# Max pooling over groups of 16: sixteen full loads, the last one pooled by four halving maxima

## The chip, the cores and the metric

The kernel runs on one core of one Trainium2 chip. The metric is device time in microseconds (us) for one execution, input and output in the chip's main memory (HBM). The engines that matter here are VectorE (DVE), which does the pooling; SyncE (SP) and ScalarE (ACT), which only issue transfers; and the 16 DMA engines, which move the bytes. On-chip memory has 128 partitions, and one instruction of DVE works on all partitions side by side.

## The reference

The reference is an adaptive max pooling of `x` with shape 32 x 256 x 4096 to 256 outputs per row. Since 4096 is a multiple of 256, every output is the maximum of 16 neighbouring values.

```python
for i in range(output_size):                      # 256
    start = int(i * length / output_size)         # 16 * i
    end = int((i + 1) * length / output_size)     # 16 * (i + 1)
    result[:, :, i] = np.max(x[:, :, start:end], axis=-1)
```

So 134.2 MB are read, 8.39 MB are written, and all values are float32.

## The kernel before, in words

All rows are one long sequence of groups of 16 values: 2,097,152 groups, 16,384 for each of the 128 partitions. A load of CHUNK = 1024 groups for each partition is 64 KB per partition and 8,192 KB in all. The sequence is cut into two large stretches, GROUPS = (9, 6): nine loads in the first, and six full loads, one load of 896 groups and one of 128 in the second. Within a stretch a partition owns consecutive groups, so that a store can take the results of many loads at once.

There is one on-chip tile `sb`. Its first RING elements hold the input of the loads, its rest the results. The ring has room for two loads, each with a gap of GAP = 152 groups beside it. Load k goes to half k % 2; every other time it is moved by the gap (`moved`, line 86). Load k+2 lies over load k but for 152 groups of it, and in their place it uses the gap. Load k is pooled in two pieces, the large one of 872 groups first and then the small one of 152 (lines 92 to 95), so load k+2 may start as soon as the large piece of load k is done. Two loads are in flight or queued at any time.

Order of the work: SP issues a short load of 128 groups (FIRST, line 70), then fifteen full loads and the last of 896 groups (line 88), all in one queue, each held back until the large piece of the load two before it is pooled. DVE pools in the same order, each piece by one `reduce_max` over the 16 values (line 57). The short load is pooled first and alone (line 73); its 128 results lie right behind the place where the 896 results of the last load go (line 98), so that one store of ACT (line 100) writes the last 1024 groups of each partition. `tc.no_sync_barrier()` makes no engine wait: it only keeps the stores behind it in the order of the program. Then SP issues the two large stores (line 103), 4,608 KB for the nine loads and 3,072 KB for the six. The first can go as soon as its nine loads are pooled, so it stands in the queue right behind the last load; the second has to wait for DVE's small piece of the last full load.

There is no hand-written planner. The waits follow from the overlap of the regions of `sb`, and the order on each engine is that of the program.

Of the kernel before, what the change touches and what calls it, by code (L numbers as in the profile page):

```python
# [1 line left out]

# [4 lines left out]


@with_exitstack
def kernel(  # L10
    ctx: ExitStack,
    tc: tile.TileContext,
    x: bass.AP,
    output_size: bass.AP,
    out: bass.AP,
):
    nc = tc.nc
    P = nc.NUM_PARTITIONS
    fp32 = mybir.dt.float32

    B, C, L = x.shape
    O = int(output_size)
    assert L % O == 0, (L, O)
    W = L // O
    total = B * C * O // P
    assert B * C * O % P == 0

    xw = x.flatten_outer_dims().rearrange("r (o w) -> (r o) w", w=W)
    ow = out.flatten_outer_dims().rearrange("r o -> (r o)")
    taken = 0  # L30

    def group(n):

        nonlocal taken
        span = slice(taken * P, (taken + n) * P)
        taken += n
        return (
            xw[span].rearrange("(p n) w -> p (n w)", p=P),
            ow[span].rearrange("(p n) -> p n", p=P),
        )  # L40

    CHUNK = 1024
    GAP = 152
    FIRST = 128
    RING = 2 * (CHUNK + GAP) * W


    GROUPS = (9, 6)
    last = CHUNK - FIRST
    assert (sum(GROUPS) + 1) * CHUNK == total and last * (W + 1) <= CHUNK * W  # L50


    pool = ctx.enter_context(tc.tile_pool(name="pool", bufs=1))
    sb = pool.tile([P, RING + total - last], fp32, tag="sb", name="sb")

    def pooled(dst, at, n):
        nc.vector.reduce_max(  # L57
            out=sb[:, dst : dst + n],
            in_=sb[:, at * W : (at + n) * W].rearrange("p (n w) -> p n w", w=W),
            axis=mybir.AxisListType.X,  # L60
        )

    groups = [
        group((loads + (g == len(GROUPS) - 1)) * CHUNK) for g, loads in enumerate(GROUPS)
    ]
    assert taken == total
    x_end, o_end = groups[-1]
    cut = GROUPS[-1] * CHUNK

    nc.sync.dma_start(  # L70
        out=sb[:, CHUNK * W : (CHUNK + FIRST) * W], in_=x_end[:, (cut + last) * W :]
    )
    pooled(RING, CHUNK, FIRST)

    rows, stores = [], []
    at = RING + FIRST
    for (xg, og), loads in zip(groups, GROUPS):
        rows += [(xg, k * CHUNK, CHUNK, at + k * CHUNK) for k in range(loads)]
        if loads:
            stores.append((og[:, : loads * CHUNK], sb[:, at : at + loads * CHUNK]))  # L80
        at += loads * CHUNK
    rows.append((x_end, cut, last, None))

    for k, (xg, a, n, dst) in enumerate(rows):

        moved = k // 2 % 2
        at = k % 2 * (CHUNK + GAP) + moved * GAP
        nc.sync.dma_start(
            out=sb[:, at * W : (at + n) * W], in_=xg[:, a * W : (a + n) * W]
        )  # L90
        if dst is not None:
            mid = CHUNK - GAP if moved else GAP
            parts = [(0, mid), (mid, n)]
            for u, v in parts if moved else parts[::-1]:
                pooled(dst + u, at + u, v - u)
        else:
            assert (at + CHUNK) * W == RING
            pooled(RING - n, at, n)

    nc.scalar.dma_start(out=o_end[:, cut:], in_=sb[:, RING - last : RING + FIRST])  # L100
    tc.no_sync_barrier()
    for dst, src in stores:
        nc.sync.dma_start(out=dst, in_=src)


# [1 line left out]
_INS = ['x', 'output_size']  # L107
_OUTS = [((32, 256, 256), 'float32')]

_NUMBERS = {'output_size': 256}  # L110


# [26 lines left out]
```

## Time and profile before

| | us |
|---|---|
| median of 3 runs | 334.76 (334.68 to 334.80) |
| the profiled execution, its own time | 334.95 |
| its span, first to last instruction | 333.2 |
| DVE busy | 276.5 |
| first landing (short load, 1,024 KB), after its issue at 0.72 | 5.0 |
| the last load: issued 291.39, to landing | 21.6 |
| ACT's store: issued 328.34, to landing | 4.0 |

The page gives the busy time of each engine as a share of the span, and the load of the DMA queues: q1 is SP's (17 loads and two stores), q10 ACT's (one store). Times in the trace count from the start of the span. A share of 1.00 in the DMA column means that the 16 DMA engines were busy throughout. The chain of waits follows the work that ended last back from the end, and names for every step what released it.

Cut into 40 equal slices, the span looks like this (each digit is the busy share of a slice in tenths); the pattern is one load after the other:

```profile
DVE  2009979797997979799797979979797997979994
POOL 0000000000000000000000000000000000000000
DMA  9898989899898989899898989999898989999997
```

### The profile page before, as it was taken

The page shows a single profiled execution, that of the slowest core. Times are in us where ns is not written, and L with a number is a line of the kernel's source. Part 1 is how long each engine was busy: PE and PEld are TensorE (multiplying, and loading weights), DVE is VectorE, ACT ScalarE, POOL GpSimd, SP SyncE. Part 2 cuts the span into 40 slices and gives each one's busy share as a digit, 9 for nine tenths or more (in the row PEclk, how much of TensorE's full clock was granted, in tenths as well). Part 3 has the DMA queues.
Part 4 walks back from the last instruction along what each step waited for, and adds up shares of the span by engine and source line. Part 5 has one row for each costly group of instructions (what it writes and reads, how often), then busy time and mean ns, then how long its engine had stood idle before and what let it go on. Part 6 is the DMA issues. An engine that isn't in the chain of part 4 may idle for free.

```text
span 333.2 us, 113 instructions
## 1 busy us (share of the span) xinstructions
DVE 276.5 (83%) x32; POOL 0.2 (0%) x4
## 2 busy tenths in 40 slices
DVE  2009979797997979799797979979797997979994
POOL 0000000000000000000000000000000000000000
DMA  9898989899898989899898989999898989999997
GB/s 378 378 504 378 504 378 496 386 409 472 378 504 378 504 378 496 386 409 472 378 504 378 504 378 488 393 409 472 378 504 378 504 378 488 393 456 434 396 406 323
DMA packets 2880, 142.61 MB, mean 428 GB/s; under 512 B 320, under 2 KB 320, under 8 KB 448
## 3 DMA queue, kind: packets, MB, share of 16 engines
q1 hardware_dynamic: 2736, 142.08, 98.8%
q10 hardware_dynamic: 144, 0.52, 0.4%
HBM read 134.22 MB, written 8.39 MB: 428 GB/s over the span
## 4 chain that ended last, share of the span: by engine, by line
DMA 58%; DVE 36%; DVEq 5%; issue 0%; SPq 0%
DMA sb<-in_x_dram 58%; DVE sb L57 36%; DVEq L134 5%; SPq L70 0%
## 5 line engine op out<-in xcount | busy, mean ns | idle before, releaser
L57 DVE TENSOR_REDUCE sb<-sb 128x872 f32<-128x13952 f32 (+3 forms) x32 | 276.5, 8681 | 51.8 <-DMA sb<-in_x_dram 51.8
L120 POOL MEMSET const-bfloat16-1.0<- 128x1 bf16 x1 | 0.1, 102 | 0.0
L120 POOL MEMSET const-uint8-127<- 128x1 uint8 x1 | 0.1, 101 | 0.0
L120 POOL MEMSET const-float32-0.0<- 128x1 f32 x1 | 0.1, 99 | 0.2 <-issue 0.2
L120 POOL MEMSET const-float32-1.0<- 128x1 f32 x1 | 0.1, 98 | 0.0
## 6 DMA issues: line engine op xcount, KB each, us to landing
sb<-in_x_dram SPq DMA_DIRECT2D x1, 7168.0 KB, 21.6
out_dram<-sb SPq DMA_DIRECT2D x1, 4608.0 KB, 32.1
out_dram<-sb SPq DMA_DIRECT2D x1, 3072.0 KB, 17.7
sb<-in_x_dram SPq DMA_DIRECT2D x1, 1024.0 KB, 5.0
out_dram<-sb ACTq DMA_DIRECT2D x1, 512.0 KB, 4.0
sb<-in_x_dram SPq DMA_DIRECT2D x15, 24.0
```

Source lines behind the costliest of these rows:

```text
L57: nc.vector.reduce_max(out=sb[:, dst : dst + n], in_=sb[:, at * W : (at + n) * W].rearrange("p (n w) -> p n w", w=W), axis=mybir.AxisListT ...
L120: nc = _bacc.Bacc("TRN2", target_bir_lowering=False, num_devices=1)
L134: with _tile.TileContext(nc) as tc:
```

## The change

The short load and its pooling are taken out. GROUPS becomes (9, 7), and all sixteen loads have 1024 groups. The first fifteen are pooled as before, each in two pieces by `reduce_max`. The sixteenth is pooled by the new function `halved`, as a whole and in place: a maximum of the first eight values of each group with the last eight, written over the first eight; then four with four, two with two, and one with one. The last writes the 1024 results to the first elements of the ring, which are free by then (the load lies in the second half of the ring, and the load before it does not reach down there). ACT stores these 1024 results, and SP's two stores have the same sizes as before.

```diff
--- before.py
+++ after.py
@@ -41,66 +41,65 @@
 
     CHUNK = 1024
     GAP = 152
-    FIRST = 128
     RING = 2 * (CHUNK + GAP) * W
 
-
-    GROUPS = (9, 6)
-    last = CHUNK - FIRST
-    assert (sum(GROUPS) + 1) * CHUNK == total and last * (W + 1) <= CHUNK * W
+    GROUPS = (9, 7)
+    assert sum(GROUPS) * CHUNK == total and sum(GROUPS) % 4 == 0 and CHUNK <= GAP * W
 
 
     pool = ctx.enter_context(tc.tile_pool(name="pool", bufs=1))
-    sb = pool.tile([P, RING + total - last], fp32, tag="sb", name="sb")
+    sb = pool.tile([P, RING + total - CHUNK], fp32, tag="sb", name="sb")
+
+    def taps(at, n):
+        return sb[:, at * W : (at + n) * W].rearrange("p (n w) -> p n w", w=W)
 
     def pooled(dst, at, n):
         nc.vector.reduce_max(
-            out=sb[:, dst : dst + n],
-            in_=sb[:, at * W : (at + n) * W].rearrange("p (n w) -> p n w", w=W),
-            axis=mybir.AxisListType.X,
+            out=sb[:, dst : dst + n], in_=taps(at, n), axis=mybir.AxisListType.X
         )
 
-    groups = [
-        group((loads + (g == len(GROUPS) - 1)) * CHUNK) for g, loads in enumerate(GROUPS)
-    ]
-    assert taken == total
-    x_end, o_end = groups[-1]
-    cut = GROUPS[-1] * CHUNK
+    def halved(dst, at, n):
 
-    nc.sync.dma_start(
-        out=sb[:, CHUNK * W : (CHUNK + FIRST) * W], in_=x_end[:, (cut + last) * W :]
-    )
-    pooled(RING, CHUNK, FIRST)
+        win = taps(at, n)
+        w = W // 2
+        while w > 1:
+            nc.vector.tensor_max(win[:, :, :w], win[:, :, :w], win[:, :, w : 2 * w])
+            w //= 2
+        nc.vector.tensor_max(
+            sb[:, dst : dst + n].unsqueeze(2), win[:, :, :1], win[:, :, 1:2]
+        )
 
     rows, stores = [], []
-    at = RING + FIRST
-    for (xg, og), loads in zip(groups, GROUPS):
-        rows += [(xg, k * CHUNK, CHUNK, at + k * CHUNK) for k in range(loads)]
-        if loads:
-            stores.append((og[:, : loads * CHUNK], sb[:, at : at + loads * CHUNK]))
+    at = RING
+    for loads in GROUPS:
+        xg, og = group(loads * CHUNK)
+        rows += [(xg, k * CHUNK, at + k * CHUNK) for k in range(loads)]
+        stores.append((og, at, loads * CHUNK))
         at += loads * CHUNK
-    rows.append((x_end, cut, last, None))
 
-    for k, (xg, a, n, dst) in enumerate(rows):
+    for k, (xg, a, dst) in enumerate(rows):
 
         moved = k // 2 % 2
         at = k % 2 * (CHUNK + GAP) + moved * GAP
         nc.sync.dma_start(
-            out=sb[:, at * W : (at + n) * W], in_=xg[:, a * W : (a + n) * W]
+            out=sb[:, at * W : (at + CHUNK) * W], in_=xg[:, a * W : (a + CHUNK) * W]
         )
-        if dst is not None:
+        if k < len(rows) - 1:
             mid = CHUNK - GAP if moved else GAP
-            parts = [(0, mid), (mid, n)]
+            parts = [(0, mid), (mid, CHUNK)]
             for u, v in parts if moved else parts[::-1]:
                 pooled(dst + u, at + u, v - u)
         else:
-            assert (at + CHUNK) * W == RING
-            pooled(RING - n, at, n)
 
-    nc.scalar.dma_start(out=o_end[:, cut:], in_=sb[:, RING - last : RING + FIRST])
+            assert moved
+            halved(0, at, CHUNK)
+
+    og, at, n = stores.pop()
+    nc.scalar.dma_start(out=og[:, n - CHUNK :], in_=sb[:, :CHUNK])
+    stores.append((og[:, : n - CHUNK], at, n - CHUNK))
     tc.no_sync_barrier()
-    for dst, src in stores:
-        nc.sync.dma_start(out=dst, in_=src)
+    for og, at, n in stores:
+        nc.sync.dma_start(out=og, in_=sb[:, at : at + n])
 
 
 # ---- launch: one core; inputs and outputs as the reference has them ----
```

## The prediction

> **What bounds the kernel now.** I read the page first, then the windows view for the DMA share by stage, the groups kept apart by shape, the chain of waits in order of time, and the DMA issues around both ends.
>
> The page has two rows that matter: VectorE (DVE) is busy 83% of the span, the loads' and SP's stores' queue q1 98.8%.
>
> ```profile
> span 333.2 us, 113 instructions
> DVE 276.5 (83%) x32; POOL 0.2 (0%) x4
> ...
> q1 hardware_dynamic: 2736, 142.08, 98.8%
> ```
>
> The windows view (length, DVE busy, clock, DMA share, GB/s) shows that this is not an average over different stages:
>
> ```profile
> 25.10:296.00 270.90, 241.91 (x28) 0.00 (x0) 1.00 1.00 433
> ...
> 313.00:330.00 17.00, 15.31 (x2) 0.00 (x0) 1.00 0.99 428
> 330.00:332.00 2.00, 0.00 (x0) 0.00 (x0) 1.00 0.65 262
> 332.00:333.20 1.20, 0.00 (x0) 0.00 (x0) 1.00 0.00 0
> ```
>
> From 25.10 to 330 the DMA engines never rest: 433 GB/s, so a load of 8,192 KB (8.39 MB) takes 19.35 us, which is also the distance of one landing from the next. The chain of waits seems to say otherwise (24 us of load, 14.7 of DVE, in turn):
>
> ```profile
> 257.33 14.70 DVE sb L57
> 272.02 0.02 issue
> 272.04 23.98 DMA sb<-in_x_dram
> 296.01 0.02 issue
> 296.04 16.96 DVE sb L57 x2
> ```
>
> But each load is issued while the one ahead of it still flows; of the 23.98 us the first 4.6 are queueing. The bound is the byte stream, up to about 330. Behind it comes a short tail, and the change acts there. The groups by shape give DVE's prices (busy, mean ns):
>
> ```profile
> L57 DVE TENSOR_REDUCE sb<-sb 128x872 f32<-128x13952 f32 x15 | 220.3, 14686 | 46.1 <-DMA sb<-in_x_dram 46.1
> L57 DVE TENSOR_REDUCE sb<-sb 128x152 f32<-128x2432 f32 x15 | 40.1, 2676 | 0.0
> L57 DVE TENSOR_REDUCE sb<-sb 128x896 f32<-128x14336 f32 x1 | 15.1, 15075 | 0.0
> ```
>
> The slope of the first two rows is (14686 - 2676) / (13952 - 2432) = 1.0425 ns for one input element of a partition, and 0.14 us is left over for each instruction. The last line to read is the DMA view from 330.0 to the end, by queue (packets, MB, share):
>
> ```profile
> q10 hardware_dynamic: 144, 0.52, 32.0%
> q1 hardware_dynamic: 16, 0.00, 0.2%
> ```
>
> q10 is ACT's store of the last pooled piece. It was issued at 328.34 (timeline), yet all its 144 packets lie behind 330.0, and of q1 only 16 empty ones are left there; in the window from 328.3 to 330.0 all 31 packets are q1's. So this store began just when SP's stores ran dry, and it landed 4.0 us after its issue, at 332.33. The rest, 0.83 us, is the closing sequence. DVE's tail is therefore nearly, but only just, covered by the stores' bytes.
>
> **The change part by part**, against the profiled execution (span 333.16, time 334.95; the median shown, 334.76, lies 0.19 lower, and I carry the difference over to it).
>
> *The bytes.* Loads and stores have the same bytes before and after: 1,024 KB leave the front and join the last load. That load's landing before is 291.39 (issue) + 21.6 = 312.99. After: the short load was issued at 0.72 and took 5.0 us, where 1,024 KB at the stream's rate take 2.42; so 2.58 is start-up. A full load issued at 0.72 lands at 0.72 + 2.58 + 19.35 = 22.65, fifteen more at 19.35 bring 312.90: 0.09 earlier. Bounds: as much as 0.7 earlier, if the start-up is partly a cost of the short load's small packets (1.75 to 4.75 ran at 330 GB/s; the same bytes at 433 would save 0.71), or 0.3 later, if larger first packets start worse. I take 0.09, the sum of the rows.
>
> *The short load and its pooling go.* DVE loses 2.29 us that lay in its 5.76 + 17.07 us of idle time before the first full load: worth nothing. SP loses one issue of 0.37; the first full load takes its place in the queue, counted above. Load 2 still waits for the large piece of load 0, at 22.65 + 14.70 = 37.4, while load 1 lands at 42.0: the same 4.6 us of cover for the stream.
>
> *SP's stores.* The 3,072 KB store waits for DVE's small piece of load 14; that comes 2.4 us earlier, but the store stands behind the last load and 4,608 KB in the same queue, so nothing moves. Its bytes end at 330, less 0.09.
>
> *The last pooling.* Before, it was 896 groups in 15.08 us, from 313.23 to 328.31; it started 0.25 after the landing because DVE still had load 14's small piece. After, load 14 lands 2.4 earlier and DVE waits for the last load; it starts 0.03 behind the landing, at 312.93. The four maxima write 8,192 + 4,096 + 2,048 + 1,024 = 15,360 elements. No row shows a two-operand operation; the nearest are the reductions, which take in one element in 1.0425 ns. If a maximum turns out one result in that time, the four take 15,360 x 1.0425 ns + 4 x 0.14 = 16.57 us. Bounds: 16.3, if neighbours overlap by 0.08 each as two pieces of a load do (14.69 + 2.68 busy in 17.28); below that nothing, unless a result cost less than an input element does in a reduction, for which no row speaks; above, twice the slope for all, 32.6. Each maximum needs the one before it; a wait on a finished DVE instruction cost ACT 0.03, so waits add 0.1. One reduction over the same 1,024 groups would take 17.22, so the four are worth 0.65 against that, but against the 896 groups of before they cost 1.5. I take 16.57: it ends at 329.50, 1.19 later than before. [...]
>
> *The last store.* ACT issues it at 329.53. Now it finds the engines free, since q1's data ended near 330 and a new DMA needs about 1 us before its first packet (the short load: issued at 0.72, first data at 1.75). Lower bound: 1.03 + 0.52 MB at 433 GB/s (1.21) + 0.43 from its last packet (331.9) to its landing = 2.7. Upper bound: 4.0, what it took when it had to queue. The one row of a DMA into idle engines, the short load's 5.0 less 1.21 for half the bytes, gives 3.8; I take 3.5. It lands at 333.03 against 332.33, **0.70 later**. The closing 0.83 stays.
>
> *Sum.* Span 333.16 + 0.70 = 333.86; by the median, 334.76 + 0.70 = **335.5 us**. With the bounds (landing -0.3 to +0.2, maxima -0.25 to +0.1, store -0.8 to +0.5, not all at once) this case runs from 334.7 to 336.2. Within 0.2% (0.67 us, about what a measurement of this kernel can tell from no change) it is as likely to be the same as slower.
>
> **The rivals.**
>
> *Spaced reads are dear: 336.5 us.* The last maximum reads, for each operand, one element in 16; the third reads pairs 16 apart. Every row of this trace reads without gaps, so none speaks for or against. If the last one's 1,024 results cost two element times each, 1,024 x 1.0425 = 1.07 us come on top, nothing covers them, and the time is 335.5 + 1.07 = 336.5; with the third as well it would be 338.7. [...] Against it: the stream of results is slow already, at 1 ns each, and may hide it. Chance 0.34.
>
> *The start-up was the short load's own: 333.9 us, faster.* If full-size first packets lose none of the 0.71 us, every landing comes that much earlier, the maxima end at 328.8, and the stream's end too moves up. This decides for faster only if the last store's flight is also near its lower bound of 2.7: 0.70 - 0.71 - 0.8 = -0.8, so 333.9; at 3.5 it ends in no change, 334.75. For it: 330 GB/s in the first 3 us against 433. Against it: the slow start may be that of any first access. It is also the only road to faster: no speed of DVE can beat a stream that is full until 330. Chance 0.09.
>
> *Two operands halve the rate: 351 us.* If both operands share one read, the four take 32.6, 16.0 more: 351.5. Nothing in the trace excludes it. [...]
>
> **How the numbers follow.** My forecast has 0.52: slower 0.26, same 0.25, faster 0.01. Spaced reads: slower 0.34. Start-up: faster 0.06, same 0.03. Half rate: slower 0.05. Together faster 0.07, same 0.28, slower 0.65. The range from 334.5 to 336.9 holds the forecast's own 334.7 to 336.2 and most of the spaced reads (336.5 with the same spread); left out are the half rate, the dear end of the spaced reads and the fast end of the start-up, about 0.15.
>
> **What would show it.** The last load lands at 312.9, and DVE waits some 2 us for it. Four two-operand maxima of 8.68, 4.41, 2.28 and 1.21 us, by shape; 2.3 us for the last one is the spaced-read rival, 17 for the first the half rate. The middle windows keep 1.00 and 433. ACT's store is issued at 329.5, and between the end of q1's data and q10's first packet the DMA share falls to 0 for some tenths of a microsecond, a gap that the kernel before does not have. The first load lands at 22.65; at 21.9 the start-up was the short load's. I would be wrong above all if the store's flight into idle engines is far from 3.5, or if the tail's start moves by more than 0.3.

## The result, and the profile after

The changed kernel takes 335.65 us (median of 8 runs, 335.53 to 335.95) against 334.76 of the kernel before (8 runs, 334.63 to 334.85): 0.89 us more, a ratio of 1.0027 with a 95% interval of 1.0018 to 1.0037. Slower, by a little more than can be told from no change. The profiled execution took 335.75, its span 334.0.

The windows view of the changed kernel (length, DVE busy, POOL busy, clock, DMA share, GB/s) shows the same full stream as before, and then something new:

```profile
25.10:293.70 268.60, 239.63 (x29) 0.00 (x0) 1.00 1.00 433
313.10:330.10 17.00, 16.88 (x4) 0.00 (x0) 1.00 0.99 428
330.70:331.40 0.70, 0.00 (x0) 0.00 (x0) 1.00 0.00 0
331.40:332.90 1.50, 0.00 (x0) 0.00 (x0) 1.00 0.86 350
```

The stream runs at 433 GB/s as ever. But from 330.70 to 331.40 no DMA engine moves data; only then come the 0.52 MB of ACT's store. The same stretch from 330.0 to 331.4, first in the kernel before, then in the changed one (a packet counts in the window in which it starts):

```profile
330.00:331.40 1.40, 0.00 (x0) 0.00 (x0) 1.00 0.85 348
```

```profile
330.00:331.40 1.40, 0.50 (x1) 0.00 (x0) 1.00 0.01 0
```

Before, ACT's store filled it. After, no new data starts in it: SP's last packets, started by 329.80, run out by 330.72, and the first of ACT's store starts at 331.40. DVE still works in the first half microsecond of the stretch. The chain of waits of the changed kernel says what was late (start, us, what):

```profile
289.06 23.96 DMA sb<-in_x_dram
313.02 0.03 issue
313.05 0.02 DVEq L66
313.07 0.05 issue
313.12 8.70 DVE sb L66
...
321.85 4.44 DVE sb L66
...
326.30 2.30 DVE sb L66
...
328.63 1.87 DVE sb L68
```

The last load lands at 313.02 (before: 312.95; the prediction's 312.99 came from a rounded 21.6). From there the chain is DVE alone, up to 330.50. Before, DVE ended at 328.31, by the timeline of that run:

```profile
296.04 32.27 DVE L57 TENSOR_REDUCE sb<-sb 128x872 f32<-128x13952 f32 x3 [2.08 <-DMA sb<-in_x_dram]
328.34 0.37 ACTq L100 DMA_DIRECT2D out_dram<-sb  x1
```

The groups by shape give the four maxima (busy, mean ns):

```profile
L66 DVE TENSOR_TENSOR sb<-sb 128x8192 f32<-128x8192 f32 x1 | 8.7, 8693 | 2.1 <-DMA sb<-in_x_dram 2.1
L66 DVE TENSOR_TENSOR sb<-sb 128x4096 f32<-128x4096 f32 x1 | 4.4, 4425 | 0.0
L66 DVE TENSOR_TENSOR sb<-sb 128x2048 f32<-128x2048 f32 x1 | 2.3, 2292 | 0.0
L68 DVE TENSOR_TENSOR sb<-sb 128x1024 f32<-128x1024 f32 x1 | 1.9, 1873 | 0.0
```

Three of them come out within 0.02 us of the sum, one result in 1.04 ns. The last does not: 1.87 us for 1,024 results, where the same rate gives 1.21. The page's list of DMA issues (KB, us to landing) has the third number that matters:

```profile
out_dram<-sb ACTq DMA_DIRECT2D x1, 512.0 KB, 2.6
```

ACT's store lands 2.6 us after its issue, where it took 4.0 when it had to queue.

### The profile page after: what moved, and what is told of

It is laid out like the page before. It is cut to its first block, busy times and chain, and to the rows that moved or that the text cites. A ratio compares the mean times of both kernels' runs of the same rounds, so it can differ in the third digit from the quotient of the medians.

```text
span 334.0 us, 114 instructions
## 1 busy us (share of the span) xinstructions
DVE 276.5 (83%) x34; POOL 0.2 (0%) x4
## 4 chain that ended last, share of the span: by engine, by line
DMA 62%; DVE 36%; issue 0%; SPq 0%; DVEq 0%
DMA sb<-in_x_dram 62%; DVE sb L57 31%; DVE sb L66 5%; DVE sb L68 1%; SPq L84 0%; DVEq L66 0%
## 5 line engine op out<-in xcount | busy, mean ns | idle before, releaser
L57 DVE TENSOR_REDUCE sb<-sb 128x872 f32<-128x13952 f32 (+1 forms) x30 | 259.2, 8681 | 51.8 <-DMA sb<-in_x_dram 51.8
L66 DVE TENSOR_TENSOR sb<-sb 128x8192 f32<-128x8192 f32 (+2 forms) x3 | 15.4, 5137 | 2.2 <-DMA sb<-in_x_dram 2.1
L68 DVE TENSOR_TENSOR sb<-sb 128x1024 f32<-128x1024 f32 x1 | 1.9, 1873 | 0.0
```

The costliest lines, as they stand in the source:

```text
L57: nc.vector.reduce_max(out=sb[:, dst : dst + n], in_=taps(at, n), axis=mybir.AxisListType.X)
L66: nc.vector.tensor_max(win[:, :, :w], win[:, :, :w], win[:, :, w : 2 * w])
L68: nc.vector.tensor_max(sb[:, dst : dst + n].unsqueeze(2), win[:, :, :1], win[:, :, 1:2])
```

## The experiments

**The theory.** Two things race at the end: DVE's last pooling with the store behind it, and the bytes of SP's stores. The time is set by the later one. I call it the tail theory, and DVE's tail covered while SP's bytes still run when ACT's store is ready to start. The rivals: the start of the stream without its short load is what costs (start-up theory), or the maxima as such (maxima theory).

**1. The last load pooled by one reduction** (the halving undone, the short load still gone).

```diff
-            halved(0, at, CHUNK)
+            pooled(0, at, CHUNK)
```

> Tail theory: from the point where the stores' bytes run out (q1's data ends at 330.1 to 330.7 in the changed kernel), the time follows the end of DVE's last pooling one for one. One reduction over 1024 groups costs 17.22 us by the rows (16,384 x 1.0425 ns + 0.14), where the four maxima with their waits took 17.39 (313.12 to 330.50); so the end comes 0.17 earlier, and the time is 335.5, the same as the changed kernel within the noise. Rival, start-up theory: the loss comes from the missing short load at the start (the first full load landed at 22.82, where the sum gave 22.65) and the maxima don't matter: 335.65. Rival, maxima theory: the maxima are the whole loss, and with one reduction the time falls back to 334.8.

Measured: 335.57 us (9 runs), ratio to the kernel before 1.0024 [1.0014, 1.0034]. The timeline of this run:

```profile
312.98 17.22 DVE L57 TENSOR_REDUCE sb<-sb 128x1024 f32<-128x16384 f32 x1 [2.15 <-DMA sb<-in_x_dram]
330.23 0.37 ACTq L98 DMA_DIRECT2D out_dram<-sb  x1
```

One reduction takes 17.22, the four maxima with their three waits 17.38 (313.12 to 330.50). So the halving is worth nothing here, and the maxima theory falls: without a maximum the kernel is as slow. Tail and start-up theory both fit.

**2. The maxima alone** (the kernel before, its last 896 groups pooled by the same four maxima; the lines that add `halved` to it are not shown).

```diff
-            pooled(RING - n, at, n)
+            halved(RING - n, at, n)
```

> The kernel before, with only its last 896 groups pooled by four maxima. They should take 13,440 x 1.0425 ns + 4 x 0.14 + 0.1 of waits + 0.57 for the spaced last one = 15.24 us against 15.08, so DVE ends at 328.47 instead of 328.31. Tail theory: the last store needs 0.9 us before its first packet and the engines are busy until 330.0 to 330.6, so this is still covered: 334.76, no change. Start-up theory: no change as well, since the short load is kept. Maxima theory: 335.6.

Measured: 334.78 us (11 runs), ratio 1.0001 [0.9992, 1.0010]. The end of this run:

```profile
313.10 13.60 DVE L67 TENSOR_TENSOR sb<-sb 128x7168 f32<-128x7168 f32 x3
326.73 1.66 DVE L69 TENSOR_TENSOR sb<-sb 128x896 f32<-128x896 f32 x1
328.43 0.38 ACTq L110 DMA_DIRECT2D out_dram<-sb  x1
```

DVE ended at 328.39, and in this run too ACT's store got its first packet only at 330.03, when q1 had no more data to start; to landing it took 3.8. The maxima theory falls for good.

**3. Packed pairs.** The third maximum writes its pairs without gaps, so that the last one reads every second element instead of every sixteenth.

```diff
-        while w > 1:
+        while w > 2:
...
+        two = sb[:, 4 * CHUNK : 4 * CHUNK + 2 * n].rearrange("p (n w) -> p n w", w=2)
+        nc.vector.tensor_max(two, win[:, :, :2], win[:, :, 2:4])
         nc.vector.tensor_max(
-            sb[:, dst : dst + n].unsqueeze(2), win[:, :, :1], win[:, :, 1:2]
+            sb[:, dst : dst + n].unsqueeze(2), two[:, :, :1], two[:, :, 1:2]
         )
```

> The changed kernel, but the third maximum writes its pairs packed into a free stretch of the ring, so that the last maximum reads every second element and not every sixteenth. Spaced-read theory: the last maximum falls from 1.87 us to about 1.22, DVE ends at 329.85, and by the tail theory the time is 335.0. Rival: the last maximum costs 1.87 for another reason (its one-element inner runs, or its packed output): it stays at 1.87 and the time at 335.65. Rival, start-up theory: the last maximum may fall, the time stays at 335.65.

Measured: 335.04 us (11 runs), ratio 1.0009 [1.0000, 1.0018]. The last maximum by shape:

```profile
L70 DVE TENSOR_TENSOR sb<-sb 128x1024 f32<-128x1024 f32 x1 | 1.2, 1226 | 0.0
```

It fell by 0.65 us, and the kernel's time by 0.61. So the spacing was the cause of the 0.65, and the time followed DVE's end nearly one for one. Packed, the four maxima take 16.74 us (313.09 to 329.83), 0.48 less than the one reduction. The start-up theory, which gave no change here, falls as the whole explanation.

**4. The last maximum done twice** (the second time with the same operands and result).

```diff
-        nc.vector.tensor_max(
-            sb[:, dst : dst + n].unsqueeze(2), win[:, :, :1], win[:, :, 1:2]
-        )
+        for _ in range(2):
+            nc.vector.tensor_max(
+                sb[:, dst : dst + n].unsqueeze(2), win[:, :, :1], win[:, :, 1:2]
+            )
```

> The changed kernel, with the last maximum done twice (the second writes the same results again). Tail theory: nothing covers DVE's end any more, so the time grows by the whole instruction, 1.87 + 0.03: 337.55. If some cover were left, less. Start-up theory: no change, 335.65.

Measured: 337.63 us (5 runs), ratio 1.0085 [1.0071, 1.0098]: 1.98 more than the changed kernel, or 1.86 if each is taken from the kernel before of its own series (334.88 here, 334.76 there); for an instruction of 1.87 and a wait of 0.03:

```profile
328.58 3.78 DVE L69 TENSOR_TENSOR sb<-sb 128x1024 f32<-128x1024 f32 x2
```

No cover is left at that end.

**5. The last load in two transfers**, each half with a reduction of its own.

```diff
-        nc.sync.dma_start(
-            out=sb[:, at * W : (at + CHUNK) * W], in_=xg[:, a * W : (a + CHUNK) * W]
-        )
+        for u in (0,) if k < len(rows) - 1 else (0, CHUNK // 2):
+            v = CHUNK if k < len(rows) - 1 else u + CHUNK // 2
+            nc.sync.dma_start(
+                out=sb[:, (at + u) * W : (at + v) * W], in_=xg[:, (a + u) * W : (a + v) * W]
+            )
...
-            halved(0, at, CHUNK)
+            for u in (0, CHUNK // 2):
+                pooled(u, at + u, CHUNK // 2)
```

> The changed kernel, but the last load comes as two transfers of 512 groups, each pooled by one reduction (8,192 x 1.0425 ns + 0.14 = 8.68 us), so that DVE's tail behind the last landing is halved and ends at about 321.8. Tail theory: the stream's end then sets the time, as in the kernel before, and nothing below it can be had: 334.76, give or take 0.2 for the start of the stream and the extra transfer. Start-up theory: no tail was ever the matter, 335.65. A third view, that every microsecond off DVE's tail is worth a microsecond: 327, which the full DMA rows up to 330 exclude.

Measured: 335.04 us (11 runs, 334.80 to 335.31), ratio 1.0008 [0.9999, 1.0017]. Better than the changed kernel (0.61 by the medians), not better than the one before. The expectation missed DVE's end: not 321.8 but 327.87. The timeline shows why:

```profile
293.41 34.47 DVE L57 TENSOR_REDUCE sb<-sb 128x872 f32<-128x13952 f32 x4 [2.07 <-DMA sb<-in_x_dram]
327.90 0.37 ACTq L101 DMA_DIRECT2D out_dram<-sb  x1
```

Four reductions run without a pause from 293.41: when the first half lands, DVE still has the load before it. DVE rests only 2.07 us per load, so splitting can win no more than about that. It was enough to bring the end back under cover.

**6. Half of the last pooling left out.**

```diff
-            halved(0, at, CHUNK)
+            pooled(0, at, CHUNK // 2)
```

> The changed kernel, but only 512 of the last load's 1024 groups are pooled, by one reduction of 8.68 us; the other half's pooling is left out, and the store writes what lies there. DVE then ends near 321.7, some 9 us before q1's data. Stream theory: the time is set by the end of the bytes, 2.5 us of closing behind it, and the 9 us are worth nothing: 334.8 to 335.05, as the kernels split at the end. Rival: part of DVE's tail still counts, or ACT's store among SP's stores disturbs them or helps them: more than 0.3 below 334.8 or above 335.05.

Measured: 334.97 us (11 runs), ratio 1.0007 [0.9998, 1.0016], with DVE's end at 321.74:

```profile
313.06 8.69 DVE L57 TENSOR_REDUCE sb<-sb 128x512 f32<-128x8192 f32 x1 [2.16 <-DMA sb<-in_x_dram]
321.77 0.37 ACTq L98 DMA_DIRECT2D out_dram<-sb  x1
```

Six more microseconds off DVE's tail, and nothing to tell from the split kernel (0.07). ACT's store, issued at 321.77, did not go at once: its first packet started at 325.48, its packets ran among SP's, whose last ended at 331.42, and it landed at 332.32, as late as in the kernel before (332.30). So the end of the bytes is a floor that DVE's tail can't lower.

**7. The start of the stream.** The split kernel and the half-pooled one are under cover and still stand 0.2 to 0.3 above the kernel before. I suspected the start: without a short load the first packets are of 64 KB per partition instead of 8 (up to 5.8 us the changed kernel moves its 2.10 MB in 32 packets, the kernel before in 160). So the first load was cut into 128 and 896 groups, once in the changed kernel (shown here) and once in the split one, and in a third kernel, split at the end too, into 32 and 992.

```diff
-        nc.sync.dma_start(
-            out=sb[:, at * W : (at + CHUNK) * W], in_=xg[:, a * W : (a + CHUNK) * W]
-        )
+        for u, v in ((0, CHUNK),) if k else ((0, 128), (128, CHUNK)):
+            nc.sync.dma_start(
+                out=sb[:, (at + u) * W : (at + v) * W], in_=xg[:, (a + u) * W : (a + v) * W]
+            )
```

> The changed kernel, but its first load comes as two transfers, 128 groups and 896, so that the stream opens with the small packets of the kernel before. Two-part theory: of the 0.89 that the change cost, some 0.25 are a worse start of the stream without a short transfer (the kernel with the last load split has its DVE tail covered again and still stands at 335.04, not at 334.78), and 0.6 the uncovered tail. Then this kernel stands at 335.4. Tail-only theory: no change, 335.65.

> The kernel with the last load split in two and one reduction for each half, its first load split as well into 128 and 896 groups. Two-part theory: both losses are mended, 334.78 as the kernel before, and by the cover nothing below that. Rival: what the split kernel lost against the kernel before was the extra transfer at the end, then it stays at 335.04.

> As the kernel split at both ends, but the first transfer has 32 groups instead of 128 (packets of 2,048 bytes). If small first packets are what makes the start cheap, the smaller ones do at least as well: 334.6 to 334.8. Rival: the transfer behind it then opens with large packets into engines that are hardly warm, and the start costs as much as without a short transfer: 335.04.

Measured: 335.62 us (8 runs; 1.0026 [1.0016, 1.0036]), 334.98 (11 runs; 1.0006 [0.9997, 1.0015]) and 334.94 (11 runs; 1.0004 [0.9995, 1.0014]). My two-part theory falls: a short first transfer gave the changed kernel next to nothing (335.62 against 335.65). In the split kernel the medians moved by 0.06 and 0.10, which the intervals can't tell from nothing.

What keeps the covered kernels without the old short load some 0.2 above the kernel before stays open; for each of the four the interval holds 1, so it may be less than that. One thing in the traces bears on it. In the profiled runs of these four, the pooling of the first full load starts between 22.40 and 22.73. In the kernel before and in that of experiment 2 it starts at 25.11 and 24.96, with 1,024 KB more ahead of it; less the 2.42 us that these take at 433 GB/s, that is 22.69 and 22.54. The span less this start is 310.4 to 310.6 in all six. So these six traces differ mostly in how soon the stream got going, and hardly at its end. Whether it gets going later on average without the old short load, one trace of each kernel can't tell.

**8. What spacing costs.** Fourteen more instructions, written behind the last pooling; only their durations are read, in one execution (352.44 us). In the trace the first six (spacings 1 to 16) run ahead of the last pooling, from 311.04 to 320.86, while SP's bytes stream; the others run behind it, from 338.07 on.

```diff
             halved(0, at, CHUNK)
...
+            n = 1020
+            for step in (1, 2, 3, 4, 8, 16, 32):
+                nc.vector.tensor_max(spaced(1024, 1, n), spaced(2432, step, n), spaced(2433, step, n))
+                n -= 4
...
```

> The changed kernel with fourteen more DVE instructions behind the last pooling, whose results nobody uses: two-operand maxima of about 1,000 results with both operands spaced by 1, 2, 3, 4, 8, 16 and 32 elements; one with only one operand spaced by 16; one with packed operands and an output spaced by 16; copies spaced by 1, 4 and 16; reductions spaced by 1 and 16. Only their durations are read. [...] Rival, a cost that grows with the distance: 1.22 at 1, 1.87 at 16, more at 32. Rival, the one-element inner runs are to blame: 1.87 at every spacing, 1 too.

The number of results tells the lines apart: 1020 for a spacing of 1, then 4 less for each next one, so 996 for 32; 988 is the one with its output alone spaced by 16. The rows are in order of cost:

```profile
L102 DVE TENSOR_TENSOR sb<-sb 128x996 f32<-128x996 f32 x1 | 2.1, 2061 | 0.0
...
L102 DVE TENSOR_TENSOR sb<-sb 128x1008 f32<-128x1008 f32 x1 | 1.9, 1939 | 0.0
...
L102 DVE TENSOR_TENSOR sb<-sb 128x1000 f32<-128x1000 f32 x1 | 1.8, 1832 | 0.0
L106 DVE TENSOR_TENSOR sb<-sb 128x988 f32<-128x988 f32 x1 | 1.8, 1819 | 0.0
...
L102 DVE TENSOR_TENSOR sb<-sb 128x1012 f32<-128x1012 f32 x1 | 1.5, 1493 | 0.0
L102 DVE TENSOR_TENSOR sb<-sb 128x1016 f32<-128x1016 f32 x1 | 1.2, 1216 | 0.0
L102 DVE TENSOR_TENSOR sb<-sb 128x1020 f32<-128x1020 f32 x1 | 1.2, 1212 | 0.0
```

Less the 0.14 us of an instruction (the prediction's figure for a reduction), a result costs 1.05 to 1.06 ns at spacings 1 and 2, 1.34 at 3, and 1.69 to 1.93 from 4 elements on. From there on there is no steady growth with the distance: 4 and 8 (1.79 and 1.81) cost more than 16 (1.69), but 32 costs most (1.93, 2.06 us for its 996 results), and that is not explained. The rival of a cost that grows with the distance fails on 4 and 8, the rival of the same cost at every spacing on 1 and 2. The running stream is not what made the difference: the kernel's own last maximum, with the DMA engines idle, costs 1.69 at spacing 16 as well (1,872 ns for 1,024 results). So the cost steps up between 2 and 4 elements, to 1.6 to 1.8 times that at 1 and 2; what makes the step, no run shows.

**All of them in one table.** DVE's end is the end of its last pooling; the third column is the span less that end. Both are of the profiled execution, which lies up to 0.24 us from the median (334.80 against 335.04 for the split last load).

| kernel | DVE's end | span - DVE's end | median us |
|---|---|---|---|
| half left out | 321.74 | 11.4 | 334.97 |
| split at both ends, first 32 | 327.79 | 5.2 | 334.94 |
| last load split | 327.87 | 5.1 | 335.04 |
| split at both ends | 327.99 | 5.2 | 334.98 |
| before | 328.31 | 4.9 | 334.76 |
| before, maxima | 328.39 | 4.6 | 334.78 |
| packed pairs | 329.83 | 3.5 | 335.04 |
| one reduction | 330.20 | 3.5 | 335.57 |
| changed, short start | 330.32 | 3.5 | 335.62 |
| changed | 330.50 | 3.5 | 335.65 |
| last maximum twice | 332.36 | 3.5 | 337.63 |

Where DVE ends at 329.83 or later, the third column is constant: DVE's end sets the time. Where it ends at 328.39 or earlier, the time is constant to 0.3 us, while DVE's end moves by more than six. That is the race of the tail theory. Its crossing lies between the two; the covered spans of 333.0 to 333.2 less the 3.5 put it near 329.6 (an estimate). So of the 0.89 us that the change cost, 0.6 to 0.7 are the uncovered tail (335.65 against the 334.94 to 335.04 of the covered kernels without the old short load), and the remaining 0.2 to 0.3 is what stays open under 7.

## Why the prediction was right

The direction, the place and the mechanism held: the bytes and the middle did not move, the pooling of 1,024 groups behind the last landing ended later than that of 896, the store behind it lost its cover, and an idle gap opened where the prediction put it (0.7 us). The forecast by itself held slower and no change for about equally likely, and slower it was, by 0.89. The predicted 335.5 lies 0.15 from the measured 335.65. But two terms of the sum were mis-sized and nearly cancelled, so that nearness is luck.

- *The last landing.* Predicted 312.90, measured 313.02. Right to 0.12. The first load came at 22.82, not at 22.65, and far from the 21.9 of the start-up rival. That rival would have made the kernel faster; it had the wrong sign, and a short first transfer changed nothing. (For this term the prediction first gave bounds of 0.7 earlier and 0.3 later, and in its sum took 0.3 and 0.2 without saying why; the result lies inside both.)
- *The last pooling.* Taken at 16.57 us, measured 17.38: the term that was too small by 0.81. Of that, 0.66 are the last maximum, whose elements lie 16 apart; the prediction priced its reads like reads without gaps in its sum, and gave the spaced reads to a rival (0.34) with 1.07, a size that no row of its trace showed. The rival was right that spaced reads cost, and too dear in size: 0.65 by packing the pairs. The rest is the waits of one maximum for another, 0.03 each, which the prediction had named and not added, and 0.04 in the durations of the others.
- *The start of it.* 313.12 instead of 312.93, the landing's 0.12 and 0.07 more of waiting.
- *The last store.* Taken at 3.5 us, measured 2.65 (330.54 to 333.18): too dear by 0.85. The lower bound, put together from the trace's own pieces (first packet, bytes, landing), was 2.7 and right in its total: the first packet came 0.87 after the issue instead of 1.03, the bytes took 1.43 instead of 1.21, and the landing followed 0.34 behind them instead of 0.43. I moved away from it because the one row of a DMA into idle engines, the short load at the start, pointed to 3.8. That row held the opening of the stream (330 GB/s in its first 3 us), with a full load queued right behind it; the store at the end stands alone, and 2.6 us of idle engines before it did not slow it (2.66 to landing with the last maximum done twice). What made the short load slow, no run separates.
- *Sum.* 333.86 predicted for the span, 333.97 measured: +0.19 +0.81 -0.85 and -0.04 at the closing.

So the number was better than its parts. Taken one at a time: with the store sized right and the spacing left out, the sum would have given 334.6, no change; with the spacing in and the store at 3.5, 336.1. None of the rivals' times came.

## What to carry to other kernels

When a DMA stream is full to its end, as here (433 GB/s), find out how late the last store may be ready before you touch the tail behind the last load. Here the tail cost nothing while that store was ready before the other bytes had run out (DVE's end at about 329.6, an estimate): below this crossing no faster arithmetic paid (six microseconds less, 321.74 instead of 327.87, bought nothing), and above it every tenth counted (0.65 us off the last maximum took 0.61 off the time). The tree of two-operand maxima wrote 15,360 results where the one reduction takes in 16,384 elements, and gave the saving back to one more fixed cost (0.14 us, from the rows of the reductions) and one more wait (0.03) per level and to the last level's spaced operands (0.65); write the last intermediate results without gaps (16.74 us against 17.38 here, and 17.22 for the reduction). Price a transfer from its own pieces in its own place (2.7 us for the last store, measured 2.65), not from the first transfer of the program (3.8).

## What the hardware did that I had not expected

A single operand or the output spaced by 16 elements costs as much as two spaced operands: 1.82 us for about 990 results in each case (about 0.64 over the contiguous price). Reductions pay as well (1.77 for 968 inputs spaced by 16, 1.17 for 972 without gaps), and copies, which run at 0.54 ns an element without gaps (0.67 us for 984, less the 0.14), take 0.99 for 976 at a spacing of 16. The third maximum, which reads and writes pairs 16 apart, pays next to nothing (2,292 ns with its output spaced or packed, where the rows of the reductions gave 2.28 us).
